# Attention masks moved from TensorE to VectorE, and the last key block's products made full width

## The chip, the cores and the metric

The kernel runs on one core of one Trainium2 chip. The metric is the device time of one execution in microseconds. Three runs of the kernel before gave 2064.73, 2064.99 and 2069.11 us; the median is 2064.99 us.

## The reference, cut to what matters

The program is one layer of a hybrid encoder: a normalisation, one wide projection, three token mixers side by side (latent attention "MLA", forgetting attention "FoX", a state-space scan), a gated merge, and a feed-forward block with a short convolution. The change touches only the two attentions. Both use 8 heads over 1024 positions in query blocks of 128, and both are causal, but by different rules:

```python
def blocked_attention(q, k, v, bias_mask):
    ...
        s = jnp.einsum('bqhd,bkhd->bhqk', q_blk, k).astype(jnp.float32) * scale
        p = jax.nn.softmax(bias_mask(i, s), axis=-1).astype(v.dtype)
        return jnp.einsum('bhqk,bkhd->bqhd', p, v)
# MLA: a frame sees its own chunk of 64 and all earlier ones
        allowed = (k_idx[None, :] // CHUNK) <= (q_idx[:, None] // CHUNK)
        return jnp.where(allowed, s, -jnp.inf)
# FoX: a forget bias, and a plain causal triangle
        s = s + Fq[..., :, None] - F[..., None, :]
        return jnp.where(k_idx[None, :] <= q_idx[:, None], s, -jnp.inf)
```

With query blocks of 128 and key blocks of 128, only the key block on the diagonal needs a mask. In MLA what is hidden there is one square: queries 0 to 63 do not see keys 64 to 127. In FoX it is the upper triangle.

## The kernel before, in words

Every float32 product is made of three float32r products (high by high, high by low, low by high). The stages follow each other: projections, then attention (about 418 to 929 us of the profiled span), then the scan, the merge, the output projection and the feed-forward block.

**Attention.** There are 16 heads (8 MLA, 8 FoX) and four units per head, 64 units in all. A unit is a pair of query blocks. `score_row` handles one query block, a row: it multiplies queries with keys into one or two chunks of a PSUM tile `s` (a ring of three; 192 chunks in all). On the last chunk of the row a further TensorE instruction on line 959 adds the mask: the bfloat16 identity `identb` is loaded as the stationary operand and `mmla` or `mfox`, a 128x128 bfloat16 mask of zeros and -1e30, streams past it into the last 128 columns. Then VectorE takes the negated maximum of each chunk (`nmx`, line 961), joins two of them (line 968), ScalarE takes the exponential into `pm` and sums it (line 971, which frees the `s` buffer), VectorE makes the reciprocal (lines 976 and 977), and GpSimd scales the row (line 978).

`values` runs two units later: four 128x128 blocks of `pm` (three for the last pair of key blocks) are transposed into a PSUM tile `tp` (line 1025), split into high and low parts `pth` (ScalarE, line 1030) and `ptl` (VectorE, line 1031), and multiplied with the values `vv`. `vv` holds the high part of the values in columns 0 to 63 and the low part in columns 64 to 127, so that one product makes both; output rows 0 to 63 and 64 to 127 of `o` are added at the end (copies on ScalarE, lines 1009 and 1010; sum on VectorE, line 1013). For the last key block of a unit only the second query block counts, so its products are 128 columns wide. There the kernel before uses three products with 64 stationary columns each (lines 1001 to 1003), which all write to rows 0 to 63 of `o`.

**Filling.** Between these, TensorE is given the projections for the gates and the convolution ("fill", line 866, tiles `mm`): 36 blocks of 48 products. `merge` runs several generators side by side. Each `yield` states the TensorE time that its piece is thought to take; `merge` always advances the one that is least far along, and fill is handed out in proportion to the stated time (`share`, from `cost_s` and `cost_v`). The stated time also moves a clock `clk`, and the work of VectorE is queued with `later(us, ...)` and issued in the order of the planned times. In the attention the order of TensorE and VectorE is the order in which this code issues it; that of ScalarE, GpSimd and the DMA queue is set by a scheduler.

Once the attention and the scan are through, whatever fill is left runs alone, and then the merge (tiles `ybr`) begins.

Of the kernel before, what the change touches and what calls it, by code (L numbers as in the profile page):

```python
# [42 lines left out]
def block_kernel(ctx: ExitStack, tc: tile.TileContext, x, positions, norm_mix_g, w_in, b_gate,  # L43
# [21 lines left out]
    def const(shape, dt, name):  # L65
        return (cp if name in keep else cp2).tile(shape, dt, name=name, tag=name)

    def scratch(shape, name, dt=F32):
# [41 lines left out]
    G.memset(mfox, 0.0)  # L110
    G.affine_select(out=mfox, in_=mfox, compare_op=ALU.is_ge, fill=NEG, base=0,
                    pattern=[[-1, P]], channel_multiplier=1)
    mmla = const([P, P], BF16, "mmla")
    G.memset(mmla, 0.0)
    G.memset(mmla[0:64, 64:128], NEG)

    def bcast(src, n, name, pool=None):
        t = (pool or cp2).tile([P, n], F32, name=name, tag=name, bufs=1)
# [821 lines left out]
        return [(0, c * P), (c * P, n * P)]  # L940

    def score_row(o, i, pn):
        mask = (mmla, mfox)[o.br]
        n = i + 1
        chunks = row_chunks(i)
        p_, _ = a_pm.get()
        nmx, _ = a_nmx.get()
        rs, rl = a_rs.get()
        pss = []
        qs = slice(i * P, i * P + P)  # L950
        for ci, (a, b) in enumerate(chunks):
            ps, pl = a_s.get()
            w = max(b - a, 256)
            last = ci == len(chunks) - 1
            for i_, (q_, k_) in enumerate(o.passes):
                T.matmul(ps[:, :w], q_[:, qs], k_[:, a:a + w], start=i_ == 0,  # L956
                         stop=not last and i_ == len(o.passes) - 1)
            if last:
                T.matmul(ps[:, b - a - P:b - a], identb, mask, start=False, stop=True)  # L959
            c = len(o.passes) * w / 2400  # L960
            later(c + 0.1, lambda ps=ps, ci=ci, a=a, b=b: V.reduce_max(  # L961
                nmx[:, ci:ci + 1], ps[:, :b - a], axis=AX, negate=True))
            pss.append((ps, pl))
            if not last:
                yield c
        two = len(chunks) == 2
        if two:
            later(c + 0.11, lambda: V.tensor_tensor(nmx[:, 2:3], nmx[:, 0:1], nmx[:, 1:2], op=ALU.min))  # L968
        nb = nmx[:, 2:3] if two else nmx[:, 0:1]
        for ci, (a, b) in enumerate(chunks):  # L970
            pss[ci][1][0] = later(c + 0.9 + 0.1 * ci, lambda ci=ci, a=a, b=b: A.activation(  # L971
                p_[:, a:b], pss[ci][0][:, :b - a], AF.Exp, bias=nb, accum_out=rs[:, ci:ci + 1]))

        def norm():
            if two:
                V.tensor_add(rs[:, 2:3], rs[:, 0:1], rs[:, 1:2])
            V.reciprocal(rs[:, 3:4], rs[:, 2:3] if two else rs[:, 0:1])  # L977
            G.tensor_scalar(p_[:, 0:n * P], p_[:, 0:n * P], rs[:, 3:4], 0.0, op0=ALU.mult, op1=ALU.add)  # L978

        rl[0] = later(c + 2.6, norm)  # L980
        pn.append((p_, rl))
        yield c + 0.05

    def scores(o, jp, pn):

# [3 lines left out]
    def values(o, jp, pn):  # L989
# [3 lines left out]
        def pv(kp, th, tl):  # L993
# [3 lines left out]
            if full:  # L997
                T.matmul(po, o.vv[:, k1, :], th[:, 256:512], start=False, stop=False)
                T.matmul(po, o.vv[:, k1, :], tl[:, 256:512], start=False, stop=False)
            else:  # L1000
                T.matmul(po[0:64, 128:256], o.vv[:, k1, 0:64], th[:, 256:384], start=False, stop=False)
                T.matmul(po[0:64, 128:256], o.vv[:, k1, 64:128], th[:, 256:384], start=False, stop=False)
                T.matmul(po[0:64, 128:256], o.vv[:, k1, 0:64], tl[:, 256:384], start=False, stop=False)
            T.matmul(po, o.vv[:, k0, :], tl[:, 0:256], start=False, stop=not full)

        def done():
# [43 lines left out]
            done()  # L1050

    def cost_s(jp, n=3):
        return sum(n * max(b - a, 256) / 2400 for i in (2 * jp, 2 * jp + 1) for a, b in row_chunks(i)) + 0.1

    def cost_v(jp):
        return 0.88 * jp + 0.33 + 0.39
# [725 lines left out]
```

## Time and profile before

| | |
|---|---|
| median of three runs | 2064.99 us |
| the profiled execution | 2072.75 us, its span 2071.0 us |
| granted TensorE clock, mean | 0.992 |
| TensorE busy | 2016.5 us, 97% of the span |
| VectorE busy | 1432.4 us, 69% |
| ScalarE busy | 949.4 us, 46% |
| GpSimd busy | 616.3 us, 30% |

The profiled execution is 7.8 us (0.4%) longer than the median. Times in the trace are counted from the start of its span. In the listings, PE is TensorE, PEld its weight loads, DVE VectorE, ACT ScalarE, POOL GpSimd; an entry such as `o<-pth,vv` names the tile written and the tiles read. In a timeline the first number is the start in us, the second the duration, and `x3` says that three equal instructions are merged. Matmuls overlap in their pipeline, so what one costs is read from the distance between starts, not from its duration.

### The profile page before, as it was taken

What the parts mean: (1) busy time and instruction counts of PE and PEld (TensorE: products, weight loads), DVE (VectorE), ACT (ScalarE), POOL (GpSimd) and SP (SyncE); (2) the same over time, 40 slices, a digit from 0 to 9 for tenths busy, and PEclk for the clock granted to TensorE, in tenths of its full rate; (3) what the DMA queues carried; (4) which work ended last, traced back from release to release, by engine and by line L of the source; (5) the groups of instructions that cost most, each with busy time, mean ns of one, the idle gap of its engine ahead of it and who ended that gap; (6) DMA issues with size and microseconds to landing.
All of it is one profiled execution on the core that took longest, in us unless ns stands there. A gap on an engine that the chain in (4) does not pass through costs nothing.

```text
span 2071.0 us, 28992 instructions
## 1 busy us (share of the span) xinstructions
PE 2016.5 (97%) x10250; PEld 1686.1 (81%) x10265; DVE 1432.4 (69%) x2586; ACT 949.4 (46%) x1730; POOL 616.3 (30%) x606
## 2 busy tenths in 40 slices
PE   7999899999999999999999999999899999999999
PEld 7899778788888888787778888888788888878887
DVE  7678479366667767657896355557987777775665
ACT  5555323156556666555554222323454444444432
POOL 4345233222222222210000040002654454422765
PEclk9999999999999999999999999999999999999999
DMA  5158777654434445324442665432222322329675
GB/s 167 45 172 261 260 221 233 204 146 141 118 114 115 130 131 133 100 82 135 134 134 82 215 209 166 153 124 64 77 93 80 96 78 72 102 93 345 218 232 190
DMA packets 274794, 303.62 MB, mean 147 GB/s; under 512 B 18860, under 2 KB 206520, under 8 KB 274648
## 3 DMA queue, kind: packets, MB, share of 16 engines
q1 hardware_dynamic: 274648, 301.76, 47.0%
q8 instruction: 81, 1.33, 0.3%
q14 instruction: 65, 0.53, 0.1%
HBM read 209.03 MB, written 92.67 MB: 146 GB/s over the span
## 4 chain that ended last, share of the span: by engine, by line
PE 81%; DVE 9%; DMA 4%; ACT 2%; issue 2%; POOL 1%; SPq 1%; DVEq 0%; ACTq 0%; POOLq 0%
PE mm L866 17%; PE dn L1729 10%; PE ybr L167 8%; PE ua L1397 5%; PE uc L1397 5%; PE ud L1397 5%; PE fx L167 5%; PE wo L1443 4%; PE s L956 4%; PE tp L1025 3%; PE ub L1397 2%; PE fxv L167 2%; PE q L167 1%; PE kv L167 1%; DMA att_d<-o 1%
## 5 line engine op out<-in xcount | busy, mean ns | idle before, releaser
L866 PE MATMUL mm<-hnh,wh 128*128 128x512 f32 x576 | 250.7, 435 | 0.0
L866 PE MATMUL mm<-hnh,wl 128*128 128x512 f32 x576 | 226.8, 394 | 0.0
L866 PE MATMUL mm<-hnl,wh 128*128 128x512 f32 x576 | 225.4, 391 | 0.0
L978 POOL TENSOR_SCALAR pm<-pm,rs 128x128 f32<-128x128 f32 (+7 forms) x128 | 107.9, 845 | 350.8 <-DVE rs L977 323.7
L1729 PE MATMUL dn<-dr,dr 128*128 128x512 f32 x592 | 182.1, 389 | 0.0
L1031 DVE TENSOR_TENSOR ptl<-tp,pth 128x512 fp32r<-128x512 f32 (+1 forms) x160 | 101.4, 634 | 84.7 <-ACT pth L1030 83.8
L961 DVE TENSOR_REDUCE nmx<-s 128x1 f32<-128x128 f32 (+2 forms) x192 | 105.8, 551 | 58.3 <-PE s L959 46.7
L971 ACT ACTIVATE pm<-s,nmx 128x128 f32<-128x128 f32 (+2 forms) x192 | 109.6, 575 | 56.9 <-DVE nmx L968 38.1
L1729 PEld LDWEIGHTS dn<-dr,dr 128*128 128x128 f32 x592 | 111.2, 188 | 23.0
L866 PEld LDWEIGHTS mm<-hnh,wl 128*128 128x128 f32 x576 | 108.2, 188 | 24.9
L866 PEld LDWEIGHTS mm<-hnl,wh 128*128 128x128 f32 x576 | 109.2, 190 | 18.4 <-issue 4.1
L866 PEld LDWEIGHTS mm<-hnh,wh 128*128 128x128 f32 x576 | 108.9, 189 | 17.8 <-issue 4.1
L1030 ACT ACTIVATE pth<-tp 128x512 fp32r<-128x512 f32 (+1 forms) x160 | 88.2, 551 | 70.4 <-PE tp L1025 69.6
L956 PE MATMUL s<-qk,qk 96*128 96x384 f32 (+5 forms) x480 | 118.1, 350 | 1.9 <-DMA qk<-q_l 0.9
L1308 POOL TENSOR_TENSOR mg<-mg,gl 128x512 f32<-128x512 f32 x16 | 24.9, 1558 | 306.8 <-DVE gl L1305 306.7
L1729 PE MATMUL dn<-dr 128*128 128x512 f32 x296 | 115.3, 389 | 0.0
L143 DVE TENSOR_TENSOR dr<-dr,dr 128x1024 fp32r<-128x1024 f32 x52 | 75.1, 1446 | 50.5 <-ACT dr L142 39.1
L167 PE MATMUL fx<-w5h,hnh 128*128 128x512 f32 x256 | 102.2, 399 | 2.5 <-ACT w5h L142 2.5
L167 PE MATMUL fx<-w5l,hnh 128*128 128x512 f32 x256 | 100.6, 393 | 2.0 <-DVE w5l L143 2.0
L167 PE MATMUL fx<-w5h,hnl 128*128 128x512 f32 x256 | 100.5, 393 | 0.0
L167 PE MATMUL ybr<-al,wh 128*128 128x512 f32 x256 | 99.2, 390 | 0.1
L167 PE MATMUL ybr<-ah,wl 128*128 128x512 f32 x256 | 98.3, 389 | 0.0
(502 smaller groups left out, 5820.9 us busy)
## 6 DMA issues: line engine op xcount, KB each, us to landing
dr<-act_d SPq DMA_DIRECT2D x99, 256.0 KB
wr<-in_ffn_w_up_dram SPq DMA_DIRECT2D x47, 512.0 KB
wr<-in_w_in_dram SPq DMA_DIRECT2D x36, 512.0 KB
g_d<-t SPq DMA_DIRECT2D x24, 512.0 KB
gl<-g_d SPq DMA_DIRECT2D x24, 512.0 KB
ws<-in_ffn_w_down_dram SPq DMA_DIRECT2D x22, 512.0 KB
wsum_d<-ws SPq DMA_DIRECT2D x22, 512.0 KB
act_d<-fa SPq DMA_DIRECT2D x22, 512.0 KB
```

The lines of the kernel that those rows point to most:

```text
L143: return i, le.tensor_sub(l, src, f32(h))
L167: T.matmul(ps, a(k), b(k), start=(i == 0), stop=(i == n - 1))
L866: T.matmul(ps, a[:, k, :], b[half][:, k, :], start=(k == 0 and i == 0), stop=(k == NK - 1 and i == 2))
L956: T.matmul(ps[:, :w], q_[:, qs], k_[:, a:a + w], start=i_ == 0, stop=not last and i_ == len(o.passes) - 1)
L961: later(c + 0.1, lambda ps=ps, ci=ci, a=a, b=b: V.reduce_max(nmx[:, ci:ci + 1], ps[:, :b - a], axis=AX, negate=True))
L971: pss[ci][1][0] = later(c + 0.9 + 0.1 * ci, lambda ci=ci, a=a, b=b: A.activation(p_[:, a:b], pss[ci][0][:, :b - a], AF.Exp, bias=nb, accum ...
L978: G.tensor_scalar(p_[:, 0:n * P], p_[:, 0:n * P], rs[:, 3:4], 0.0, op0=ALU.mult, op1=ALU.add)
L1030: later(c + 0.05, lambda th=th, pt=pt, off=off: A.activation(th[:, :off], pt[:, :off], AF.Copy))
L1031: pl[0] = later(c + 0.6, lambda th=th, tl=tl, pt=pt, off=off: V.tensor_sub(tl[:, :off], pt[:, :off], f32(th[:, :off])))
L1397: T.matmul(ps, a, b, start=first and n == 0, stop=n == 11, skip_group_check=not first)
L1443: T.matmul(p, a, b, start=k == 0 and i == 0, stop=k == NK - 1 and i == 2)
L1729: T.matmul(ps[m], a[:, ts_], b[:, 512:], start=first_ and j == 0 and q == 0, stop=j == NFH - 1 and q == 2, skip_group_check=not first_)
```

## The change

1. The mask product of line 959 and its weight load go (128 of each, one per row). In MLA, VectorE sets the hidden square of 64 partitions by 64 columns to -1e30 in PSUM (`memset`, 64 of them). In FoX, VectorE adds `mfox` in place to the last 128 columns (`tensor_add`, 64 of them). Both stand right ahead of the maximum of that chunk on VectorE. In the built program the maximum waits for VectorE's own count, that is for the mask to be written.
2. The row's stated time loses the 0.05 us for the mask product, and `cost_s` loses 0.1 us per unit.
3. The last key block's three products with 64 stationary columns become two with 128.
4. The constant `mmla` goes (256 bytes per partition, and two GpSimd memsets at the start), so the tiles allocated behind it lie 256 bytes lower.

```diff
-    mmla = const([P, P], BF16, "mmla")
-    G.memset(mmla, 0.0)
-    G.memset(mmla[0:64, 64:128], NEG)
...
     def score_row(o, i, pn):
-        mask = (mmla, mfox)[o.br]
...
                 T.matmul(ps[:, :w], q_[:, qs], k_[:, a:a + w], start=i_ == 0,
-                         stop=not last and i_ == len(o.passes) - 1)
-            if last:
-                T.matmul(ps[:, b - a - P:b - a], identb, mask, start=False, stop=True)
+                         stop=i_ == len(o.passes) - 1)
             c = len(o.passes) * w / 2400
-            later(c + 0.1, lambda ps=ps, ci=ci, a=a, b=b: V.reduce_max(
+            if last and o.br == 0:
+                later(c + 0.1, lambda ps=ps, e=b - a: V.memset(ps[0:64, e - 64:e], NEG))
+            elif last:
+                later(c + 0.1, lambda d=ps[:, b - a - P:b - a]: V.tensor_add(d, d, mfox))
+            later(c + 0.101, lambda ps=ps, ci=ci, a=a, b=b: V.reduce_max(
                 nmx[:, ci:ci + 1], ps[:, :b - a], axis=AX, negate=True))
...
-        yield c + 0.05
+        yield c
...
             else:
-                T.matmul(po[0:64, 128:256], o.vv[:, k1, 0:64], th[:, 256:384], start=False, stop=False)
-                T.matmul(po[0:64, 128:256], o.vv[:, k1, 64:128], th[:, 256:384], start=False, stop=False)
-                T.matmul(po[0:64, 128:256], o.vv[:, k1, 0:64], tl[:, 256:384], start=False, stop=False)
+                T.matmul(po[:, 128:256], o.vv[:, k1, :], th[:, 256:384], start=False, stop=False)
+                T.matmul(po[:, 128:256], o.vv[:, k1, :], tl[:, 256:384], start=False, stop=False)
...
-        return sum(n * max(b - a, 256) / 2400 for i in (2 * jp, 2 * jp + 1) for a, b in row_chunks(i)) + 0.1
+        return sum(n * max(b - a, 256) / 2400 for i in (2 * jp, 2 * jp + 1) for a, b in row_chunks(i))
```

How the instructions stand, on the two engines that the prediction speaks of. First TensorE, at the end of the second unit of the first head (MLA), before: the last score product of a row, the mask, the last key block's products, and what stands ahead of the next unit's first product.

```order
L956 MATMUL s_5366<-qk_1037_5061,qk_1040_5064 128x256
L959 LDWEIGHTS identb
L959 MATMUL s_5366<-mmla,identb 128x128
L996 MATMUL o<-pth_5240,vv_5059 128x256
L1001 MATMUL o<-pth_5240,vv_5059 64x128
L1002 MATMUL o<-pth_5240,vv_5059 64x128
L1003 MATMUL o<-ptl_5241,vv_5059 64x128
L1004 MATMUL o<-ptl_5241,vv_5059 128x256
L1025 MATMUL tp_5382<-ident,pm_5132 128x128
L1025 MATMUL tp_5382<-ident,pm_5167 128x128 x2
L866 MATMUL mm_5353<-hnh_128,wh_5080 128x512
```

The same place in the changed kernel (its lines are numbered a few lower):

```order
L952 MATMUL s_5362<-qk_1037_5058,qk_1040_5061 128x256
L994 MATMUL o<-pth_5236,vv_5056 128x256
L999 MATMUL o<-pth_5236,vv_5056 128x128
L1000 MATMUL o<-ptl_5237,vv_5056 128x128
L1001 MATMUL o<-ptl_5237,vv_5056 128x256
L1022 MATMUL tp_5377<-ident,pm_5128 128x128
L1022 MATMUL tp_5377<-ident,pm_5163 128x128 x2
L994 MATMUL o<-pth_5308,vv_5056 128x256
```

The mask and its load are gone, three narrow products are two full ones, and at this place the six fill products that stood between the transpositions and the next unit's first product (the one of line 996 before, 994 now) have moved elsewhere. Such a unit border without fill, where at most seven short instructions stand between a unit's last product and the next unit's first, is found 10 times among the 63 borders before and 12 times now. Of the fill's 1728 products, 1090 stand inside the attention before and 1061 now; behind the scan, alone, stand 36 before and 66 now.

Second VectorE, in the first head, before (the maximum of a row's last chunk, the joined maximum, and the work around it):

```order
L829 SCALAR_TENSOR_TENSOR t_1019_5050<-t_1014_4998,pc_g,t_1019_5050 128x509
L961 TENSOR_REDUCE nmx_5197<-s_5228 128x1
L968 TENSOR_TENSOR nmx_5197<-nmx_5197 128x1
L1031 TENSOR_TENSOR ptl_5241<-tp_5236,pth_5240 128x384
L961 TENSOR_REDUCE nmx_5256<-s_5258 128x1
```

and the same row now:

```order
L956 MEMSET s_5225 64x64
L959 TENSOR_REDUCE nmx_5193<-s_5225 128x1
L966 TENSOR_TENSOR nmx_5193<-nmx_5193 128x1
L826 SCALAR_TENSOR_TENSOR t_1019_5047<-t_1014_4995,pc_g,t_1019_5047 128x509
L1028 TENSOR_TENSOR ptl_5237<-tp_5232,pth_5236 128x384
L959 TENSOR_REDUCE nmx_5253<-s_5255 128x1
```

One instruction more per row stands ahead of the maximum (in FoX, line 958, it is the addition of `mfox`), and here the row has moved one place ahead of a convolution step.

## The prediction

> **What bounds the kernel now.** I read the page's busy shares and its chain first, then the stage in which the change lies.
>
> ```profile
> PE 2016.5 (97%) x10250; PEld 1686.1 (81%) x10265; DVE 1432.4 (69%) x2586; ACT 949.4 (46%) x1730; POOL 616.3 (30%) x606
> PE 81%; DVE 9%; DMA 4%; ACT 2%; issue 2%; POOL 1%; SPq 1%; DVEq 0%; ACTq 0%; POOLq 0%
> ```
>
> TensorE is busy for 97% of the span and carries 81% of the chain. The attention stage alone, by windows (length, then busy time of PE, PEld, DVE, ACT, POOL):
>
> ```profile
> 405.00:930.00 525.00, 513.21 (x3048) 432.91 (x3047) 351.96 (x792) 307.18 (x767) 124.13 (x143) 1.00 0.44 121
> 740.00:765.00 25.00, 24.98 (x149) 20.78 (x147) 20.59 (x49) 15.92 (x41) 7.10 (x8) 1.00 0.52 149
> ```
>
> TensorE idles for 12 of 525 us; the granted clock is 1.00. VectorE is at 67% (352 of 525), and up to 82% in 25 us (20.59). What TensorE waits for, from the waits of the stretch 418 to 930 us (total, times, longest):
>
> ```profile
> PE o L996 <- ACT o L1010: 9.8, 12, 2.1
> PEld s L956 <- ACT pm L971: 2.7, 5, 0.8
> PE s L956 <- ACT pm L971: 0.9, 2, 0.6
> DVE nmx L961 <- PE s L959: 46.7, 51, 11.2
> ```
>
> 9.8 of the 12 us are waits of a unit's first product for the copies of the unit before out of `o`. For a score buffer, the end of the chain that the change lengthens, TensorE hardly waits (0.9 us). VectorE on its side waits for TensorE (46.7 us). So TensorE sets the pace, and an instruction less on it shortens the stage by its slot.
>
> **The mask product's slot.** The recorded duration is no price, since matmuls overlap:
>
> ```profile
> L959 PE MATMUL s<-mmla,identb 128*128 128x128 bf16 x64 | 14.8, 231 | 0.0
> ```
>
> I price it by starts, in pairs with and without it ahead of the same work. Ahead of transpositions:
>
> ```profile
> 617.66 0.69 PE L956 MATMUL s<-qk,qk 96*128 96x384 f32 x3
> 618.19 0.49 PE L1025 MATMUL tp<-ident,pm 128*128 128x128 f32 x3
> ...
> 607.21 0.69 PE L956 MATMUL s<-qk,qk 96*128 96x384 f32 x3
> 607.74 0.23 PE L959 MATMUL s<-mmla,identb 128*128 128x128 bf16 x1
> 607.81 0.61 PE L1025 MATMUL tp<-ident,pm 128*128 128x128 f32 x4
> ```
>
> Three score products take 0.53 us to the next start both times (618.19-617.66; 607.74-607.21); with the mask the transposition starts 0.07 us later. Ahead of value products and of fill the mask also delays the instruction behind the next one:
>
> ```profile
> 594.33 0.23 PE L959 MATMUL s<-mmla,identb 128*128 128x128 bf16 x1
> 594.37 0.36 PE L996 MATMUL o<-pth,vv 128*128 128x256 f32 x1
> 594.57 0.22 PE L1001 MATMUL o<-pth,vv 128*64 128x128 f32 x1
> ...
> 617.18 0.28 PE L996 MATMUL o<-pth,vv 128*128 128x256 f32 x1
> 617.30 0.28 PE L998 MATMUL o<-pth,vv 128*128 128x256 f32 x1
> ...
> 423.23 0.23 PE L959 MATMUL s<-mmla,identb 128*128 128x128 bf16 x1
> 423.27 0.48 PE L866 MATMUL mm<-hnh,wh 128*128 128x512 f32 x1
> 423.58 0.39 PE L866 MATMUL mm<-hnl,wh 128*128 128x512 f32 x1
> 423.82 0.39 PE L866 MATMUL mm<-hnh,wl 128*128 128x512 f32 x1
> ```
>
> The mask's own slot is 0.04 us, and the first product behind it occupies 0.20 us (594.57-594.37) where 0.12 is normal (617.30-617.18): 0.12 us together. With fill it is 0.04 plus 0.31 instead of 0.24: 0.11 us. In the timeline of the stage the mask stands ahead of a transposition 44 times, ahead of a value product 42, a score product 30, fill 12 (128). I take 0.07 us for the 44 and 0.12 us for the other 84, the score products priced like the value products: 3.1 + 10.1 = 13.2 us. Bounds: 9.0 us at 0.07 for all, 15.4 at 0.12 for all. A gain of nothing would need TensorE to wait elsewhere instead; that is a rival below.
>
> **The last key block's products.** Before, three with 64 stationary columns:
>
> ```profile
> 612.06 0.22 PE L1001 MATMUL o<-pth,vv 128*64 128x128 f32 x1
> 612.24 0.33 PE L1004 MATMUL o<-ptl,vv 128*128 128x256 f32 x1
> 612.40 0.39 PE L956 MATMUL s<-qk,qk 96*128 96x512 f32 x1
> ```
>
> The three take 0.18 us (0.06 each), and the full-width product behind them 0.16 instead of 0.12: 0.34 us. Two full-width products with 128 streamed columns do not occur in this stage; the nearest are those of the scan, eight in a row with 128 stationary columns and 128 or 64 streamed:
>
> ```profile
> 1008.63 0.22 PE L1199 MATMUL py<-xdt,Eh 128*128 128x128 f32 x1
> 1009.44 0.36 PE L1168 MATMUL pcb<-bc 128*128 128x128 f32 x1
> ```
>
> 0.81 us for eight, 0.10 each, although they stream half as much as the 0.12 us products or less: the slot follows the stationary width, not the streamed columns. By that row the new end is 2x0.10 + 0.12 = 0.32 against 0.34 us: 0.02x64 = 1.3 us gained; at 0.12 each it is 0.36, 1.3 us lost. If streamed columns alone counted, two at 0.06 and one at 0.12 would be 0.24: 0.10x64 = 6.4 us gained. I take 0, being between the two nearest rows, and keep -6.4 to +1.3.
>
> [...]
>
> **VectorE's new instructions.** No in-place mask stands in the trace; the nearest rows read the same PSUM tile:
>
> ```profile
> L961 DVE TENSOR_REDUCE nmx<-s 128x1 f32<-128x128 f32 x16 | 4.6, 287 | 12.6 <-PE s L959 12.6
> L961 DVE TENSOR_REDUCE nmx<-s 128x1 f32<-128x256 f32 x32 | 13.5, 421 | 10.4 <-PE s L959 10.2
> ...
> 686.70 0.56 DVE L961 TENSOR_REDUCE nmx<-s 128x1 f32<-128x384 f32 x1 [1.58 <-PE s L959]
> 687.29 0.16 DVE L968 TENSOR_TENSOR nmx<-nmx 128x1 f32<-128x1 f32 x1
> ```
>
> 128 columns more cost 134 ns, so 128 columns cost 0.29 us and 64 about 0.22 (287-67); the floor is the 0.16 us of a one-column operation. A dependent instruction starts 0.03 us behind its predecessor's end (686.70+0.56 to 687.29). So 64x(0.29+0.03) + 64x(0.22+0.03) = 36 us more on VectorE at most, 128x0.16 = 20 us at least. With 352 + 36 of 525 - 13 us it is 76% busy: still covered by TensorE. Per row the maximum comes 0.25 to 0.32 us later, less the 0.07 us by which the scores are ready sooner. Behind it in VectorE's order stand the `ptl` splits and the convolution steps; the exponential on ScalarE waits for it, and the score buffer is freed by that. The cover is the ring of three score buffers:
>
> ```profile
> L961 DVE TENSOR_REDUCE nmx<-s x192: 283/552/693, 421.0 to 908.2; 128x1 f32<-128x384 f32 x80, 128x1 f32<-128x512 f32 x64, 128x1 f32<-128x256 f32 x32, 128x1 f32<-128x128 f32 x16
> ...
> 609.47 0.20 ACT L971 ACTIVATION_READ_ACCUMULATOR pm<-s,nmx 128x1 f32 x1
> ```
>
> 192 chunks in 487 us are one per 2.54 us, so a buffer comes round every 7.6 us; the chunk whose scores began at 607.21 (above) left its buffer at 609.67, 2.5 us later. I allow 1 us of new waits for them (the 3.6 us that TensorE and its loads wait now, grown by a quarter); with the cover gone the price is in the third rival.
>
> **The moved fill.** 29 fill products leave the attention and run behind the scan. At 0.23 us (423.82-423.58, rounded down) that is 7 us from one dense stretch to another, sum 0. But fill also covers the wait for `o`:
>
> ```profile
> 605.54 0.49 PE L1025 MATMUL tp<-ident,pm 128*128 128x128 f32 x3
> 606.63 0.39 PE L996 MATMUL o<-pth,vv 128*128 128x256 f32 x1 [0.60 <-ACT o L1010]
> ```
>
> A border with three transpositions and no fill costs 0.60 us. The order has 12 borders without fill instead of 10: +1.2 us.
>
> **The sum**: -13.2 + 0 + 1.0 + 1.2 = -11.0 us. The profiled execution (2072.75 us, span 2071.0) becomes 2061.8; against the median of 2064.99 the same step gives 2054.0 us, own range 2047 to 2059.
>
> **The rivals.**
>
> *Products priced by streamed columns alone*: 6.4 us more, 2047.6 us. For it, the three narrow products do run at 0.06 us; against it, the 0.10 us of the scan's. Chance 0.10.
>
> *The stage is paced by the exchange with ScalarE, and the slots come back as waits*: TensorE gets to the next unit's first product sooner, but the copy out of `o` (0.60 us behind its release now) and the exponentials come no sooner. If 9 to 13 us come back, the time is 2061 to 2066, say 2064 us. For it, ScalarE's copies already hold TensorE 12 times; against it, 51 of 63 borders have no such wait. Chance 0.12.
>
> *VectorE falls behind and the score ring holds TensorE*: slower. The place is the chain from the score product over mask and maximum to the exponential. It decides once a chunk's exponential ends more than 7.6 us behind its scores, against the 2.5 us read above. In the stretch of 82% VectorE has 4.4 us idle in 25; six rows there add 6x0.29 = 1.7 us. If that tips over into row-by-row locking, each row is longer by 0.18 to 0.25 us, 23 to 32 us in all, less the 13.2: +10 to +19, say 2079 us. Against it, TensorE's 0.9 us of waits for `pm` today. [...] Chance 0.08.
>
> *The 256-byte shift of all later tiles changes durations*: no row can price it; it would show in groups that the change leaves alone. Chance 0.04, either sign.
>
> **How the numbers follow.** The forecast has 0.66; its time is 2054. A measurement of this kernel tells about 0.2%, 4.1 us, from no change, so faster means below 2060.9, slower above 2069.1. Faster: 0.66 + 0.10 + 0.02 of the shift + 0.02 of the paced case = 0.80. Same: 0.10 of the paced case + 0.02 = 0.12. Slower: 0.08. The range 2046 to 2065 holds the streamed-column case, the bounds of the mask's slot (9.0 to 15.4) and most of the paced case.
>
> **What would show it.** Right: line 959 gone, TensorE's idle time in the attention still 10 to 15 us, the stage (418.9 to about 929) shorter by some 18 us, of which 7 return behind the scan; 0.20 to 0.24 us between the start of the last key block's first full-width product and the one behind the second; VectorE 20 to 36 us busier there. Wrong: new waits `s <- ACT pm` of more than 5 us (third rival), `o <- ACT o` above 15 us (second), the two products at 0.12 us together (first), or unchanged groups such as `wl` on line 815 with other durations.

## The result, and the profile after

The changed kernel is slower. Its runs gave 2079.57, 2083.41, 2083.96 and 2087.54 us, median 2083.68; the kernel before, beside them, 2067.05 us. The ratio is 1.0085 with a 95% interval of 1.0069 to 1.0102, so 16.6 us more. The prediction said 2054 us, and its range ended at 2065.

The page of the changed kernel (2079.57 us, span 2077.8 us), its busy line and its chain:

```profile
PE 2007.9 (97%) x10058; PEld 1685.3 (81%) x10073; DVE 1444.6 (70%) x2714; ACT 951.5 (46%) x1730; POOL 618.1 (30%) x604
...
PE 75%; DVE 11%; DMA 6%; ACT 3%; issue 2%; POOL 1%; SPq 1%; another core or an unknown queue 0%; ACTq 0%; DVEq 0%; POOLq 0%
```

TensorE is busy for 8.6 us less than before (2007.9 against 2016.5), yet the span is 6.8 us longer. Its share of the chain falls from 81 to 75%, and VectorE, DMA and ScalarE take it over. So TensorE's work became less, and something else stretched the span. Where, the starts and ends of the stages tell (first score product, first transposition `stp`, last one, first product `ybr` of the merge, end; us):

| stage | before | after | difference |
|---|---|---|---|
| ahead of the attention | 419.1 | 412.5 | -6.6 |
| attention, to the first `stp` | 515.5 | 505.1 | -10.4 |
| scan, first to last `stp` | 209.7 | 228.9 | **+19.2** |
| from there to the merge (fill alone) | 8.0 | 14.8 | +6.8 |
| merge to the end | 918.7 | 916.5 | -2.2 |

The first row differs between profiles of kernels whose TensorE order is the same there (412.5 to 419.4 us), so it is no effect; the profile before has 10.2 us at a clock of 0.50 between 90 and 105 us that the other lacks. A product into `kv` took 0.43 us there (starts at 102.34 and 102.77) and 0.23 behind it (104.67 and 104.90); over the 9.5 us of it in which TensorE was busy that is by estimate 4.4 of the 6.6 us. The attention is shorter and the moved fill returns behind the scan, both as predicted in kind, but the attention only by 10.4 us, of which the 30 moved products (at 0.23 us) are 6.9, where some 18 were forecast. The loss lies in the scan, where the change touches no line.

The windows of the attention (405 to 930 us) and of the scan (930 to 1160 us), of the changed kernel (length, then busy time of PE, PEld, DVE, ACT, POOL, then granted clock, DMA share, GB/s):

```profile
405.00:930.00 525.00, 507.64 (x2877) 434.03 (x2877) 380.66 (x936) 314.35 (x776) 129.16 (x143) 1.00 0.46 125
930.00:1160.00 230.00, 216.75 (x1067) 169.92 (x1081) 162.71 (x323) 107.48 (x172) 0.00 (x0) 0.96 0.36 111
```

and the scan's window of the kernel before:

```profile
930.00:1160.00 230.00, 228.29 (x1154) 179.32 (x1169) 176.41 (x342) 116.58 (x186) 0.00 (x0) 1.00 0.43 130
```

In the scan TensorE idled for 1.7 us before (230 less 228.29) and idles for 13.3 now, and its granted clock is 0.96 instead of 1.00. What it waits for, from the waits of the stretch (total, times, longest), after:

```profile
PE stp L1239 <- ACT y L1231: 11.1, 5, 3.1
PE py L1196 <- DVE y L1200: 1.3, 1, 1.3
```

and before:

```profile
PE stp L1242 <- ACT y L1234: 0.5, 1, 0.5
PE py L1199 <- PE pse L1176: 0.4, 1, 0.4
```

The transposition of a finished scan chunk waits for ScalarE's last step on it, the scaling of `y` by the root of its mean square. Windows of 20 us show the clock's part (the clock is the third number from the end; two of the ten windows):

```profile
1012.00:1032.00 20.00, 16.84 (x76) 12.12 (x76) 14.57 (x30) 8.87 (x15) 0.00 (x0) 0.91 0.25 78
1032.00:1052.00 20.00, 17.16 (x85) 14.28 (x85) 13.67 (x32) 9.04 (x15) 0.00 (x0) 0.84 0.34 108
```

Between 1012 and 1112 us the clock is 0.91, 0.84, 0.91, 1.00 and 0.91; (0.09+0.16+0.09+0.09) x 20 us is 8.6 us of clock lost. These are means: narrower windows of the same trace show 0.50 for 3.4 us from 1021.6, for 10.2 us from 1045.5 and for 3.4 us from 1100.1, and 1.00 between them. At 0.50 a fill product took 0.43 us (starts at 1048.38 and 1048.81), at 1.00 it took 0.23 (1058.50 and 1058.73). In some 1.7 us of these 17 TensorE was waiting anyway; over the other 15.3 the slow clock cost by estimate 7.1 us. With the 11.5 us of waits that are new (12.4 less 0.9) that makes 18.6 of the 19.2 us.

In the attention the waits did grow (after; before it was `o` 9.8 and, on the loads, `s` 2.7):

```profile
PE o L994 <- ACT o L1007: 15.1, 14, 2.3
...
PEld s L952 <- ACT pm L969: 8.9, 27, 0.6
```

**The chain in the scan.** ScalarE squares `y` to get the sum for the root, and writes the squares, which nobody reads, into `yT`, a single buffer that still holds the transposed chunk before. So the square has to wait until that chunk's store (`ys_d`) has left it. ScalarE's timeline, one scan chunk, before:

```profile
1013.32 0.59 ACT L1243 ACTIVATE yT<-stp 128x512 f32<-128x512 f32 x1
...
1017.41 1.06 ACT L1229 ACTIVATE yT<-y 128x1024 f32<-128x1024 f32 x1 [0.80 <-DMA ys_d<-yT]
...
1029.55 1.14 ACT L1234 ACTIVATE y<-y,yr 128x1024 f32<-128x1024 f32 x1
```

and the same chunk after:

```profile
999.26 0.59 ACT L1240 ACTIVATE yT<-stp 128x512 f32<-128x512 f32 x1
...
1005.38 1.07 ACT L1226 ACTIVATE yT<-y 128x1024 f32<-128x1024 f32 x1 [1.48 <-DMA ys_d<-yT]
...
1018.57 1.13 ACT L1231 ACTIVATE y<-y,yr 128x1024 f32<-128x1024 f32 x1
```

From the start of the last copy into `yT` to the square's start it is 4.1 us before (1017.41-1013.32) and 6.1 after; from VectorE's product that finishes `y` (1012.37 before, 998.32 after) to the scaling 17.2 and 20.2 us. VectorE's timeline shows another delay in it, after:

```profile
1006.56 0.15 DVE L1228 TENSOR_SCALAR yv<-yss 128x1 f32<-128x1 f32 x1 [0.39 <-ACT yT L1226]
1007.51 1.23 DVE L812 TENSOR_TENSOR wl<-wr,wh 128x1024 fp32r<-128x1024 f32 x1 [0.80 <-ACT wh L811]
1008.66 0.15 DVE L145 TENSOR_SCALAR rs_i<-yv 128x1 int32<-128x1 int32 x1
```

Between the mean square and the first step of its root VectorE waits 0.80 us for a weight of the fill and then splits it for 1.23 us. Before, that split stands elsewhere in the chunk (1026.26 us). Both can come from the fill. Each scan chunk is given 11.0 us of it (the changed kernel's `FILL_SSD`), which is one block: 48 products at 0.23 us, with a load of 512 KB, a store and a split. So the place in the chunk at which a block begins stays nearly the same from chunk to chunk, and the 30 products that the changed stated times left behind moved that place. The 1164 products ahead of the scan before are 24 blocks of 48 and 12 products, the 1134 now are 23 blocks and 30. This was the theory for the first experiments.

### The profile page after: what moved, and what is told of

Same layout as the page of the kernel before. It is cut to its first block, busy times and chain, and to the rows that moved or that the text cites. A ratio compares the mean times of both kernels' runs of the same rounds, so it can differ in the third digit from the quotient of the medians.

```text
span 2077.8 us, 28775 instructions
## 1 busy us (share of the span) xinstructions
PE 2007.9 (97%) x10058; PEld 1685.3 (81%) x10073; DVE 1444.6 (70%) x2714; ACT 951.5 (46%) x1730; POOL 618.1 (30%) x604
## 3 DMA queue, kind: packets, MB, share of 16 engines
q8 instruction: 79, 1.29, 0.3%
## 4 chain that ended last, share of the span: by engine, by line
PE 75%; DVE 11%; DMA 6%; ACT 3%; issue 2%; POOL 1%; SPq 1%; another core or an unknown queue 0%; ACTq 0%; DVEq 0%; POOLq 0%
PE mm L863 14%; PE ybr L164 8%; PE dn L1726 8%; PE ua L1394 5%; PE uc L1394 5%; PE fx L164 5%; PE ud L1394 5%; PE wo L1440 4%; PE s L952 4%; DMA att_d<-o 3%; PE ub L1394 2%; PE tp L1022 2%; PE fxv L164 1%; PE q L164 1%; PE kv L164 1%
## 5 line engine op out<-in xcount | busy, mean ns | idle before, releaser
L976 POOL TENSOR_SCALAR pm<-pm,rs 128x128 f32<-128x128 f32 (+7 forms) x128 | 113.1, 886 | 339.6 <-DVE rs L975 219.0
L959 DVE TENSOR_REDUCE nmx<-s 128x1 f32<-128x128 f32 (+2 forms) x192 | 106.4, 554 | 13.3 <-PE s L952 8.6
```

What stands on the lines that cost most here:

```text
L959: later(c + 0.101, lambda ps=ps, ci=ci, a=a, b=b: V.reduce_max(nmx[:, ci:ci + 1], ps[:, :b - a], axis=AX, negate=True))
```

## The experiments

A stated time is what a piece of work gives in its `yield`; it sets how much fill is handed out, not what runs. The times of the kernel before beside the runs were 2067.3 to 2068.0 us in the median.

**The scan: is it the phase of the fill?** Four kernels, each with or without the masks, and with 1164 or 1134 fill products ahead of the scan.

```diff
 # the changed kernel with the old stated times
-        yield c
+        yield c + 0.05
-        return sum(...)
+        return sum(...) + 0.1
```

> The changed kernel with the stated times of the kernel before (0.05 us per row and 0.1 us per unit put back), so that 1164 fill products instead of 1134 are handed out ahead of the scan, as before the change; masks and full-width products stay as changed. Theory (phase): the scan's time depends on where in a scan chunk a block of fill begins, and the 30 fewer fill products have moved that. Then the scan (first to last transposition of stp) takes about 210 us again instead of 228.9, TensorE's waits in it are below 4 us, and the time is about 2055 us, 0.5% below the kernel before. Rival (masks): the masks and products themselves, or the 256-byte shift, disturb the scan: it stays at about 229 us and the time at about 2080 us, 0.7% above the kernel before.

Measured 2067.57 us (10 runs), ratio 0.9998 (0.9985 to 1.0011). The scan took 209.4 us.

```diff
 # the kernel before with the new stated times, and nothing else
-        yield c + 0.05
+        yield c
-        return sum(...) + 0.1
+        return sum(...)
```

> The kernel before with nothing but the changed stated times: the masks stay on TensorE, the three narrow products and the constant stay, and 1134 fill products stand ahead of the scan. Theory (phase): the scan takes about 229 us, TensorE waits 10 us or more in it for the scaling of y, and the time is 15 to 20 us above the kernel before (about 2083 us). Rival (masks): the scan stays at about 210 us and the time within 3 us of the kernel before.

Measured 2095.46 us (4 runs), ratio 1.0131 (1.0109 to 1.0154). The scan took 228.5 us.

```diff
 # the changed kernel, more fill ahead of the attention
-            merge([], 11.0)
+            merge([], 17.5)
```

> The changed kernel with its new stated times, but 6.5 us more fill handed out ahead of the attention (17.5 instead of 11.0), so that again 1164 fill products stand ahead of the scan while the attention holds 1061 as in the changed kernel. Theory (phase): scan about 210 us, time about 2055 us, as with the old stated times. Rival (the distribution of fill inside the attention, or the state in which the attention leaves the other engines, decides): scan about 229 us, time about 2080 us.

Measured 2082.42 us (4 runs), ratio 1.0071 (1.0054 to 1.0088). The scan took 212.2 us.

```diff
 # the kernel before, less fill ahead of the attention
-            merge([], 11.0)
+            merge([], 4.0)
```

> The kernel before with 7 us less fill handed out ahead of the attention (4.0 instead of 11.0), so that 1134 fill products stand ahead of the scan as in the changed kernel; masks, products and stated times are those before. Theory (phase): scan about 229 us with 10 us or more of TensorE's waits for the scaling of y, time 15 to 20 us above the kernel before. Rival (masks, or stated times by another way than the phase): scan about 210 us, time within 3 us of the kernel before.

Measured 2087.52 us (4 runs), ratio 1.0093 (1.0069 to 1.0117). The scan took 223.2 us.

The waits of the scan's transpositions in the profiles with the new stated times only:

```profile
PE stp L1242 <- ACT y L1234: 10.2, 5, 2.8
```

and with less fill:

```profile
PE stp L1242 <- ACT y L1234: 10.5, 5, 3.1
```

All four scans went with the number of fill products ahead of them (209.4 and 212.2 us with 1164; 228.5 and 223.2 with 1134), whatever the masks were. The masks, the products and the constant's 256 bytes have no part in it: the kernel with the new stated times only has the masks where they were, and its scan is as slow. So the theory of the phase holds for the scan, as far as two starting points can show it; no other was run.

It does not hold for the whole of the time. With more fill ahead the scan was nearly back, and yet the kernel was at 2082 and not at 2055 us. In its profile (2078.66 us, the fastest of the four) the attention is 2.6 us shorter than before, though 6.9 us of fill left it, so 4.3 us longer for its work, and the scan 2.5 us longer. TensorE waits 22.7 us in this attention (11.8 before). The two longest waits are 4.2 us for a score buffer and 3.6 us for `o`. The clock is below 1.00 in two of the eight windows of this stage, 0.98 from 430 to 500 us (6.6 us idle) and 0.95 from 710 to 780 (5.3 us idle); from 850 to 930 us it is 1.00 with 5.1 us idle. So the fill's place seems to matter in the attention too. The other runs' mean granted clock was 0.988 to 0.990, against a mean of 0.994 in the 13 runs of the kernel before; 0.005 of 2067 us is 10 us, an estimate of what it cost. Those three runs have no profile, so what lowers their clock further stays open. And the old stated times alone did not bring 2055 us either, but exactly the time before: the masks and products gain nothing there. That is the second question, below.

**The scan: is the chain what the phase acts through?**

```diff
 # the changed kernel; the squares go to zt, which is free when y is done
-            A.activation(o.yT.rearrange("p j s -> p (j s)"), yf, AF.Square, accum_out=ss)
+            A.activation(zt, yf, AF.Square, accum_out=ss)
```

> The changed kernel with one edit in the scan: the square whose row sum gives the scale of y (line 1226) writes its elements, which nobody reads, into zt instead of yT. In the changed kernel that instruction waits 3.3 to 5.5 us behind the last copy into yT, until the store of yT (ys_d) has left it; zt is free when y is. The fill and its phase stay as in the changed kernel (1134 products ahead of the scan). Theory (the phase acts through the chain from y to its scaling, which has no slack because of the store): the chain becomes 2 to 6 us shorter in every chunk, TensorE's waits for the scaling of y (11.1 us) go, the clock of the scan with them, the scan takes 208 to 212 us instead of 228.9, and the time is 2062 to 2068 us. Rival (the phase acts through something else, VectorE's order or the fill's own work): the scan stays above 222 us and the time above 2076 us.

Measured 2070.98 us (10 runs), ratio 1.0014 (1.0003 to 1.0025): 12.7 us of the changed kernel's loss gone, by an edit that moves no work. The time is 3 us above the range that was expected. The scan took 212.2 us. Its window in the profile:

```profile
930.00:1160.00 230.00, 226.64 (x1157) 177.93 (x1156) 174.15 (x335) 115.21 (x185) 0.00 (x0) 1.00 0.42 126
```

and its waits:

```profile
PE stp L1239 <- ACT y L1231: 2.3, 2, 1.2
```

The clock is at 1.00 again although the fill begins where it did in the changed kernel. From the finished `y` to its scaling it is 14.0 us in the chunk that took 20.2. ScalarE's idle time ahead of that line, in the view of the line's instructions, was in the changed kernel

```profile
  DMA ys_d<-yT: 11.4, 6
```

and in the kernel before

```profile
  DMA ys_d<-yT: 8.1, 6
```

With the squares moved the entry is gone. So the chain is the way in which the phase reaches TensorE. It does not follow that the store is what the phase made longer. By the timelines, the second to the sixth chunk take 15.4 us in the mean from the finished `y` to its scaling before, 18.3 in the changed kernel and 15.1 here. Up to the square's start these are 4.5, 5.6 and 1.5 us; from the root's first step (`rs_i`) to the scaling, where VectorE does the root's steps in between other work, they are 8.1, 10.1 and 10.8. The store was thus waited for before as well, and only some 1 us of the 2.9 that the chain grew lies there; the rest lies in VectorE's order. Moving the squares takes 4 us off each chunk, more than the chain had grown. The split of the fill's weight was not tried alone; its 1.23 us are read from the timeline only.

**The attention: what do the masks and the products gain?** All with the old stated times, so that the fill before the scan is as it was.

```diff
 # the kernel before with the full-width products only
-                T.matmul(po[0:64, 128:256], o.vv[:, k1, 0:64], th[:, 256:384], ...)   # and two more
+                T.matmul(po[:, 128:256], o.vv[:, k1, :], th[:, 256:384], ...)         # and one more
```

> The kernel before with nothing but the full-width products of the last key block (masks on TensorE, old stated times, constant kept). By the slots read in the changed kernel's trace (the products and the one behind them 0.29 us instead of 0.34, 64 times) 3.2 us less: ratio to the kernel before about 0.9985. Rival (a faster TensorE only waits longer for the copies out of o): ratio 1.000, with the waits of o for ACT 3 us longer.

Measured 2067.61 us (12 runs), ratio 0.9998 (0.9986 to 1.0011), and `o` waits 9.7 us, as before. The expectation's 0.29 us was a misreading. The timeline of the changed kernel has

```profile
612.39 0.22 PE L999 MATMUL o<-pth,vv 128*128 128x128 f32 x1
612.45 0.28 PE L1000 MATMUL o<-ptl,vv 128*128 128x128 f32 x1
612.56 0.33 PE L1001 MATMUL o<-ptl,vv 128*128 128x256 f32 x1
612.73 0.40 PE L863 MATMUL mm<-hnh,wh 128*128 128x512 f32 x1
```

and from the first to the start behind the wide one it is 0.34 us (612.73-612.39), the same as the 0.34 before. Over the 64 places without a visible wait the mean is 348 ns before and 344 ns in this run. The products are worth nothing: slots of 0.06, 0.11 and 0.17 us sum to what three of 0.06 and one of 0.16 did.

```diff
 # the kernel before with the masks on VectorE only (old stated times, narrow products)
-            if last:
-                T.matmul(ps[:, b - a - P:b - a], identb, mask, start=False, stop=True)
+            if last and o.br == 0:  V.memset(the hidden square)
+            elif last:              V.tensor_add(the last 128 columns, mfox)
```

> The kernel before with nothing but the masks on VectorE (old stated times, narrow products; the constant goes). By the slots 6.4 us less on TensorE for the masks themselves. Theory (VectorE's part comes back as waits for the score ring, the third rival of the prediction in a small form): waits s for pm and o for o are 4 to 7 us longer than before and the ratio to the kernel before is 1.000 to 1.002. Rival (the masks gain as predicted and the products lose): ratio 0.994 to 0.997.

Measured 2065.11 us (12 runs), ratio 0.9983 (0.9973 to 0.9993): 2.8 us gained, between the theory and the rival. The waits:

```profile
PEld s L952 <- ACT pm L969: 12.7, 25, 1.8
...
PE o L994 <- ACT o L1008: 12.3, 14, 2.7
...
PE s L952 <- ACT pm L969: 4.6, 4, 1.3
```

TensorE's starts, taken together from the first score product to the scan with visible idle time left out, fell from 503.7 to 492.9 us, which is 10.8 us less. Of that, at most 1.6 us are by estimate the clock's: the profile before has 3.4 us at 0.50 in the attention, from 862.1 us, where a fill product took 0.43 us (starts at 862.30 and 862.73) instead of 0.23. So at least 9 us of slots are gained, and 5.3 us of visible waits (11.8 to 17.1 us) come back. The slots still hold what the weight loads wait for score buffers, 12.7 us here against 2.7 before.

```diff
 # the changed kernel, old stated times, no mask on any engine
-            if last and o.br == 0: ...
-            elif last: ...
```

> The changed kernel with the old stated times, and the masks left out on every engine (so hidden positions take part). It prices VectorE's masks: against the same kernel with them (2067.6 us, as before the change). Theory (the 26 us of mask instructions on VectorE delay the exponentials and cost TensorE the gain): 6 to 10 us less than with the masks, ratio to the kernel before 0.995 to 0.997, waits s for pm back to 3 us. Rival (TensorE's own speed brings the waits, since the copies of o and the exponentials come no sooner): ratio 0.999 to 1.000.

Measured 2056.53 us (6 runs), ratio 0.9939 (0.9922 to 0.9955): 11.4 us below the kernel before and 11.0 below the same kernel with its masks on VectorE, a little more than the 6 to 10 that were expected. The waits:

```profile
PE o L990 <- ACT o L1003: 12.5, 12, 3.0
...
PEld s L952 <- ACT pm L965: 3.4, 6, 1.0
...
PE s L952 <- ACT pm L965: 1.5, 3, 0.8
```

With the masks on VectorE and all else the same (the first of the experiments, old stated times) the last two were

```profile
PEld s L952 <- ACT pm L969: 12.4, 24, 1.8
PE s L952 <- ACT pm L969: 4.6, 4, 1.3
```

The waits for the score buffers are back near what they were, those for `o` are not. So with the old stated times TensorE gains what was predicted, and VectorE's masks, together with the full-width products, give it back, mostly through the score buffers. The longer waits for `o` (2.7 us more than before) belong to the faster TensorE: that much of the rival's mechanism is there.

This price does not hold wherever the fill stands. With the new stated times alone the time was 2095.46 us, and with the masks and products added, which is the changed kernel, 2083.68 us: 11.8 us less (by the two ratios 9.5). There TensorE itself waited only 0.4 us for the score buffers, and its loads 8.9 us in 27 waits of at most 0.6 us. So the steps do not add: the same two edits gain nothing with the old stated times and some 10 us with the new ones. Why VectorE's masks cost less there was not tried.

```diff
 # no masks; the same amount of VectorE work behind the row's maximum, to a spare tile
+        V.tensor_copy(dum[0:64, 0:64], s[0:64, last 64 columns])    # MLA
+        V.tensor_add(dum, s[:, last 128 columns], mfox)             # FoX
```

> The changed kernel with the old stated times, in which VectorE does as much work on the same columns of s as the masks are, but writes it to a spare tile and does it behind the row's maximum (behind the joined maximum, where there is one) instead of ahead of it; the masks themselves are left out, so hidden positions take part. It separates the two ways in which VectorE's masks can cost TensorE 11 us. Theory (the row's own chain: mask, maximum, exponential, score buffer): the exponential is as early as without masks, so the time is that of the kernel without masks, 2056 to 2059 us, ratio 0.994 to 0.996. Rival (VectorE's occupancy: whatever stands behind is late by so much): the time is that with masks, 2065 to 2068 us, ratio 0.999 to 1.000.

Measured 2060.51 us (6 runs), ratio 0.9967 (0.9954 to 0.9979). It lies between the two: VectorE's occupancy costs 4.0 us (2060.5 less 2056.5), and that the mask stands ahead of the maximum, in the row's own chain, another 7.1 (2067.6 less 2060.5). By the ratios, each to its own runs of the kernel before, the two are 5.8 and 6.4 us, and each time has an interval of about 3 us to either side; so both take part, and which is larger is not shown. The stand-ins weigh a little more than the masks:

```profile
L967 DVE TENSOR_TENSOR dum<-s,mfox 128x128 bf16<-128x128 f32 x64 | 18.0, 281 | 0.0
...
L965 DVE CAST dum<-s 64x64 bf16<-64x64 f32 x64 | 13.3, 207 | 0.0
```

**Which mask?** The groups of the changed kernel's masks on VectorE (busy, mean ns, idle before):

```profile
L958 DVE TENSOR_TENSOR s<-s,mfox 128x128 f32<-128x128 f32 x64 | 18.8, 293 | 16.4 <-PE s L952 16.1
...
L956 DVE MEMSET s<- 64x64 f32 x64 | 7.2, 112 | 25.8 <-PE s L952 25.0 <-ACT t L868 0.3
```

FoX's addition takes 0.293 us, MLA's setting of a square 0.112 us. On TensorE the two do not differ before: 231 ns of recorded duration each, and from the mask's start to the next one 0.07 us ahead of a transposition and 0.04 ahead of any other product, in MLA and in FoX.

```diff
 # changed kernel, old stated times, squares to zt; FoX's mask stays on TensorE
-            elif last:
-                V.tensor_add(d, d, mfox)
+            if last and o.br: T.matmul(ps[:, b - a - P:b - a], identb, mfox, start=False, stop=True)
```

> The changed kernel with the old stated times and the square of the scan written into zt, in which only MLA's mask is set on VectorE (0.112 us each in the changed kernel's trace, 64 times); FoX's mask stays a product on TensorE. Theory (VectorE's mask instructions give back what TensorE gains, and FoX's additions are most of them: 18.8 of 26.0 us): half of the masks' slots and the products gain about 7 us on TensorE and VectorE's 7.2 us cost about 3, so 4 us below the kernel before: ratio 0.998, waits s for pm between those before (0.9 us) and those with both masks on VectorE (4.6 us). Rival (any mask on VectorE costs its row the same, since it is one more dependent step): ratio 1.000.

Measured 2061.28 us (7 runs), ratio 0.9967 (0.9952 to 0.9981). That is below the 0.998 that was expected. This version beats both kernels: 6.7 us below the one before, 22 below the changed one. Its waits:

```profile
PE o L994 <- ACT o L1007: 11.1, 13, 2.6
...
PEld s L952 <- ACT pm L969: 7.0, 14, 1.7
...
PE s L952 <- ACT pm L969: 2.1, 3, 1.3
```

> The changed kernel with the old stated times, in which only FoX's mask is added on VectorE; MLA's stays a product on TensorE (the constant too). Theory (each mask costs by its time on VectorE, 0.293 us in FoX and 0.112 in MLA): FoX's is not worth moving; with the products' 3 us the ratio to the kernel before is 0.999 to 1.001, against 0.9967 with MLA's alone. Rival (both masks gain alike, and only their sum on VectorE is too much): ratio 0.996 to 0.998.

Here the edit is the other way round (MLA's mask on TensorE, FoX's on VectorE, the squares where they were). Measured 2069.99 us (12 runs), ratio 1.0016 (1.0005 to 1.0027), a little above the theory's 1.001 and far from the rival's range. The two masks are not alike: MLA's is worth moving, FoX's is not. The squares' place differs between these two kernels too, but without waits in the scan it had nothing to gain (scans of 208.8 and 209.7 us).

**A lever that failed.** GpSimd is idle in the scan (0.00 of 230 us) and busy for a quarter of the attention (129 of 525 us), so it was given VectorE's split of the fill's weights.

```diff
 # changed kernel, old stated times, squares to zt
-        rl[0] = later(5.3, lambda: V.tensor_sub(l, raw, f32(h)))
+        rl[0] = later(5.3, lambda: G.tensor_sub(l, raw, f32(h)))
```

> The changed kernel with the old stated times and the square of the scan written into zt; both masks on VectorE, but the low part of the fill's weights (line 812, wl, 23 times 1.29 us of VectorE in the attention) is made by GpSimd, which is busy for a quarter of the attention and not at all in the scan. Theory (the masks cost TensorE because VectorE's other work delays them; 30 us less of that outweighs their 26): the gain of the kernel without masks comes back in most part, 6 to 10 us below the kernel before, ratio 0.995 to 0.997. Rival (the price is the row's own longer chain of dependent steps, 0.14 to 0.32 us, whatever else VectorE has to do): ratio 0.999 to 1.001.

Measured 2080.57 us (6 runs), ratio 1.0060 (1.0046 to 1.0073). With MLA's mask alone on VectorE the same:

> Both edits together: only MLA's mask on VectorE, and wl made by GpSimd (old stated times, the square into zt). Theory: VectorE has 23 us less to do in the attention than before the change; 6 to 8 us below the kernel before, ratio 0.996 to 0.997. Rival: ratio 0.999 to 1.000.

Measured 2083.43 us (6 runs), ratio 1.0069 (1.0055 to 1.0084). The groups of GpSimd in the attention of the first:

```profile
L812 POOL TENSOR_TENSOR wl<-wr,wh 128x1024 fp32r<-128x1024 f32 x23 | 55.3, 2406 | 53.4 <-ACT wh L811 53.4
```

The split takes 2.41 us there instead of VectorE's 1.29, and GpSimd waits 53.4 us for ScalarE ahead of it with the scaling of the rows (`pm`) queued behind. TensorE's waits for `pm` on the transpositions and for the score buffers grew:

```profile
PEld s L952 <- ACT pm L969: 18.1, 31, 2.0
...
PEld tp L1022 <- POOL pm L976: 2.9, 3, 2.1
```

Both times miss theory and rival. Ahead of the attention time was lost as well: 423.5 and 425.9 us in the two, against 412.5 to 419.4 in the kernels with VectorE's split and the same fill there, and in the first TensorE idled for 34.2 of the first 415 us, against 28.4 with both masks and the split on VectorE and the old stated times. It says nothing on whether VectorE's occupancy or the row's chain is the price, since it brought a new wait of its own.

## Why the prediction was wrong, point by point

- **The moved fill, sum 0: this is the step that failed.** "29 fill products leave the attention and run behind the scan. At 0.23 us that is 7 us from one dense stretch to another." The 7 us did move (+6.8 behind the scan). What the step left out is the stretch between: the scan holds exactly one block of fill per chunk, beside a chain that was just in time (0.5 us of waits for it before). The 30 products moved the block's place in every chunk: +19.2 us, 11.5 of waits and by estimate 7.1 of granted clock. The prediction read the waits of the stretch from 418 to 930 us only and listed no rival that lay behind it.
- **The mask product's slot, -13.2 us: right.** Without masks on any engine, 11.4 us were gained (ratio 0.9939), within the bounds of 9.0 to 15.4; with the masks on VectorE the slots fell by at least 9 us, net of what the loads newly wait.
- **The last key block's products, 0: right.** 0.34 us before and after, and a ratio of 0.9998 alone. The mean of 0.10 us was read from eight products of the scan whose own slots, in the same rows of the trace, run from 0.06 to 0.14. The two prices from which the 0 was taken do not hold singly: the first full-width product takes 0.06 us, no more than a narrow one, so the slot did not follow the stationary width here; the second takes 0.11. The time from the first to the start behind the second is 0.17 us, outside the 0.20 to 0.24 given as its mark; the wide product behind them, at 0.17, makes up for it. What sets the 0.06 and the 0.11 apart no run shows.
- **VectorE's new instructions, 20 to 36 us, covered for +1.0 us: the size of the work right, the cover wrong with the fill where it was.** The masks take 26.0 us of VectorE (18.8 and 7.2), within the 20 to 36, though MLA's 0.112 us is below the 0.16 that was taken as the floor. With the old stated times that gave back 11.0 us and not 1.0. The third rival named the mechanism, the score ring, and put it at 0.08 with row-by-row locking of 23 to 32 us; in truth it is a partial loss. The cover was read as a mean, 2.5 us of a ring of 7.6, and the mean hides the late rows: with the masks the loads wait for score buffers 24 times instead of 5, 12.4 us in all, none longer than 1.8 us. This step alone would have missed too: with the fill where it was, the time is 2067.57 us, above the 2065 at which the range ended.
- **The `o` borders, +1.2 us: under-sized.** `o` waits are 15.1 us instead of 9.8, above the 15 us that was to speak for the second rival. In the kernel with only the new stated times they are 14.6 us, with the masks where they were, so most of that too comes from the fill's place.
- **The 256-byte shift: no effect seen.** The unchanged kernel with new stated times shows the slow scan without it.

Summed by the medians: slots about -11, VectorE's part +11, so 0 with the fill where it was (2067.6); then +16 from the stated times (2083.7), of which 12.7 go when the squares leave `yT`. The other way round, the stated times alone are +28 (2095.5) and the masks and products then -12, close to the -11.0 of the sum. Either way it is the moved fill, put at 0, that makes the kernel slower, by 16 to 28 us; what the masks gain depends on it, and how is open.

## What to carry to other kernels

A change in the stated cost of a step is a change of its own wherever such costs hand out work: count what it moves, and check every later stage where the moved work runs beside a chain without slack, not just the stage that was edited. A buffer used as a dump for values that nobody reads carried that buffer's waits here (11.4 us of ScalarE for the store of `yT`); sending them to another tile took 12.7 us off the changed kernel. An engine at 70% is not a cover by its mean: price an added step on it by whether it stands ahead of something that frees a buffer, and move only the cheap one (0.112 us against 0.293).

## What the runs showed of the hardware that was not expected

In the changed kernel's scan the granted clock fell along with short waits: with 11.1 us of waits for `y`, none longer than 3.1 us, 20-us windows were granted 0.84 to 0.91; with 2.3 us of them, by the squares' move alone, the windows of the same stretch were at 1.00. Inside those windows the clock was at 0.50 for 3.4 to 10.2 us at a time and at 1.00 otherwise, and each such spell began within 2 us of the end of a wait (1.9 us behind it, 1.1 and 0.7 us ahead of it): of the scan's five waits for `y`, those of 3.1, 2.8 and 2.4 us had one, those of 1.8 and 1.1 us had none. Here 11.5 us of waits went with 19 us of time. That is no fixed price: with less fill, 10.5 us of such waits, none longer than 3.1 us, left the window from 930 to 1160 us at 0.99, where the changed kernel had 0.96, and with more fill a single one of 2.8 us left it at 1.00. And a product of one shape did not have one slot: at the last key blocks the first full-width product with 128 streamed columns took 0.05 to 0.07 us, the second, ahead of one with 256, 0.10 to 0.12; among the eight products of the scan those with 128 streamed columns took 0.06 us once and 0.14 three times.
